# The end of a hybrid decoder layer: part of the last scaling moved to a product with a diagonal matrix

## The chip, the cores and the metric

The kernel runs on one core of a Trainium2 chip. The metric is the time of one execution on the device in microseconds (us), as the median of several runs. Durations of single instructions come from one profiled execution, which has a time of its own.

## What is computed

A decoder layer for 256 tokens of 2048 channels: pre-norm, one wide input projection, two token mixers (a gated delta rule and a block attention), two branch projections merged by gates, an output projection, a post-norm and the residual. What the change touches is the last line alone:

```python
        y = hybrid_mixer(h, w_in[l], ...)          # ends in merged @ w_out
        x = x + rms_norm(y, post_norm_w[l])        # rms_norm: y * rsqrt(mean(y*y) + 1e-6) * w
```

Per token, all 2048 values of y are needed for the mean before any value of the output can be formed.

## The kernel before, in words

The 256 tokens are two tiles of 128 (`t` = 0, 1; a token is a partition). The output projection is cut into four column blocks of 512 (`c` = 0 to 3). Each weight tile is split into a high and a low part of the reduced-precision fp32 form that TensorE takes in one pass, and each product of fp32 operands is three such products (high by high, high by low, low by high); line 147 is the helper that issues all of them. Blocks 0 to 2 are partly formed in combined products earlier; block 3 is plain: for each tile, 16 steps of the contraction by three products, all of tile 0 and then all of tile 1.

**The banks.** Products land in PSUM banks of 128x512 fp32. `acc_tile` takes one from a pool of four, `aux_tile` one from another pool of four. At the end the four `acc` banks hold `c11`, `c21` (block 0, tiles 0 and 1) and `c12`, `c22` (block 1). Block 2 stands in two `aux` banks. Block 3 asks the `acc` pool for two more tiles, `pts`, so these get banks that an earlier block has left; the tile framework adds whatever waits that needs.

**weigh(c, t)** (L1211) reads a finished block twice: ScalarE squares it and sums along the row into `ssy[t][:, c]` (L1214), then VectorE multiplies it by the post-norm weight into `yw[t]` in SBUF (L1215). The two readers of one bank run one behind the other: VectorE's product waits for ScalarE's Square. Blocks 0, 2 and 1 are weighed in this order, the last ones when block 3's weights are already split and kept in SBUF (`keep`, L1246).

**so_far(t)** (L1217) sums the squares of the first three blocks ahead of time.

**finish(t)** (L1224) comes after `weigh(3, t)`: ScalarE takes the root (L1226), VectorE the reciprocal (L1227), and then VectorE goes over the 2048 columns in five pieces (256, 512, 512, 512, 256), each `yw * rs + x` (L1231), with x loaded earlier as `hx`. Behind each piece stands a store to HBM (L1235), in turn on SP's and on ScalarE's DMA queue. For tile 0 this lies beside TensorE's work on tile 1; for tile 1 nothing follows.

**Order.** `mm`, and everything wrapped in `pin`, stays in program order on its engine. Each engine is a queue in order: an instruction that waits holds up all that stand behind it, and a store issued on a queue waits there for its data.

Of the kernel before, what the change touches and what calls it, by code (L numbers as in the profile page):

```python
# [8 lines left out]
F32 = mybir.dt.float32  # L9
F32R = mybir.dt.float32r  # L10
BF16 = mybir.dt.bfloat16
AF = mybir.ActivationFunctionType
ALU = mybir.AluOpType
AX = mybir.AxisListType

P = 128
EPS = 1e-6
# [57 lines left out]
def hybrid_layer(  # L75
# [15 lines left out]
    nc = tc.nc  # L91
    B, S, D = x.shape
    NT = S // P
# [7 lines left out]
    of = out.rearrange("b s d -> (b s) d")  # L101
# [14 lines left out]
    wk = ctx.enter_context(tc.tile_pool(name="wk", bufs=2))  # L116
# [7 lines left out]
    def acc_tile(name):  # L124
        return acc.tile([P, 512], F32, tag="acc", name=name)
# [18 lines left out]
    pin = tc.keep_in_program_order  # L144

    def mm(*args, **kwargs):
        return pin(nc.tensor.matmul(*args, **kwargs))  # L147
# [19 lines left out]
    for c in range(NCH):  # L167
        for t in range(NT):
            cs = slice(c * 512, (c + 1) * 512)
# [7 lines left out]
    ident = cst.tile([P, P], F32, name="ident")  # L177
    make_identity(nc, ident)
    rstd = cst.tile([P, NT], F32, name="rstd")
# [936 lines left out]
    for blk in ORDER:  # L1116
        n, c = blk[:2].rstrip("0123456789"), int(blk[-1])
# [88 lines left out]
    yw = [big.tile([P, D], F32, tag=f"z{t}", name=f"yw_{t}") for t in range(NT)]  # L1206
    hx = big.tile([P, NT, D], F32, tag="g1", name="hx")
    nc.gpsimd.dma_start(hx, xf.rearrange("(t p) d -> p t d", p=P))
    ssy = [cst.tile([P, 4], F32, name=f"ssy_{t}") for t in range(NT)]

    def weigh(c, t, pt):  # L1211
        jy = wk.tile([P, 512], BF16, tag="jy", name=f"jy_{c}_{t}")
        cs = slice(c * 512, (c + 1) * 512)
        pin(nc.scalar.activation(jy, pt, AF.Square, accum_out=ssy[t][:, c : c + 1]))  # L1214
        pin(nc.vector.tensor_tensor(yw[t][:, cs], pt, postw[:, cs], op=ALU.mult))  # L1215

    def so_far(t):  # L1217

        rb = wk.tile([P, 2], F32, tag="mx", name=f"rb_{t}")[:, 0:1]
        pin(nc.vector.tensor_reduce(rb, ssy[t][:, 0:3], axis=AX.X, op=ALU.add))  # L1220
        pin(nc.vector.tensor_scalar(rb, rb, 1.0 / D, EPS, op0=ALU.mult, op1=ALU.add))
        return rb

    def finish(t, rb):  # L1224
        rs = wk.tile([P, 1], F32, tag="rstd", name=f"rs_{t}")
        pin(nc.scalar.activation(rs, ssy[t][:, 3:4], AF.Sqrt, bias=rb, scale=1.0 / D))  # L1226
        pin(nc.vector.reciprocal(rs, rs))  # L1227
        for i, (c0, c1) in enumerate(((0, 256), (256, 768), (768, 1280), (1280, 1792), (1792, D))):
            cs = slice(c0, c1)
            pin(  # L1230
                nc.vector.scalar_tensor_tensor(  # L1231
                    yw[t][:, cs], yw[t][:, cs], rs, hx[:, t, cs], op0=ALU.mult, op1=ALU.add
                )
            )
            (nc.sync if i % 2 == 0 else nc.scalar).dma_start(of[t * P : (t + 1) * P, cs], yw[t][:, cs])  # L1235

    mq.drain()

# [19 lines left out]
    for c, banks in ((0, (c11, c21)), (1, (c12, c22))):  # L1258
        for h in range(2, 4):
            product([quarter(0, h), quarter(1, h)], load(wo, h, c, "y"), banks, [False, False], f"y{c}_{h}")  # L1260
            if h == 2:
                last_parts(c)
        for t in range(NT):
            weigh(2 * c, t, (pts2 if c else banks)[t])
    c = 3
# [3 lines left out]
    for t in range(NT):  # L1269
        weigh(1, t, (c12, c22)[t])  # L1270
    rbs = [so_far(t) for t in range(NT)]
    for t in range(NT):
        for k in range(KT):
            hi, lo = parts[k // 2][0][:, k % 2], parts[k // 2][1][:, k % 2]
            sh = mT[:, k, t * P : (t + 1) * P]
            sl_ = mT[:, k, S + t * P : S + (t + 1) * P]
            mm(pts[t], sh, hi, start=(k == 0), stop=False)
            mm(pts[t], sh, lo, start=False, stop=False)
            mm(pts[t], sl_, hi, start=False, stop=(k == KT - 1))
        weigh(c, t, pts[t])  # L1280
        finish(t, rbs[t])


# [26 lines left out]
```

## Time and profile before

| | us |
|---|---|
| median of 3 runs | 773.82 (773.29 to 774.91) |
| the profiled execution, its own time | 774.99 |
| its span, first to last instruction | 773.2 |
| TensorE products busy | 762.8 |
| VectorE busy | 563.5 |
| ScalarE busy | 433.7 |
| GpSimd busy | 34.6 |

The span is what the profiler saw between the first and the last instruction; the execution's time is 1.8 us longer. In rows of a timeline the first column is the start and the second the duration, both in us; `PE` is TensorE, `PEld` its weight loads, `DVE` VectorE, `ACT` ScalarE, and `SPq` and `ACTq` are the queues on which DMAs are issued. In brackets stands how long the engine had been idle and who released it. In rows of groups the last columns are the summed time in us, the mean of one in ns, and the idle time before.

### The profile page before, as it was taken

The page shows a single profiled execution, that of the slowest core. Times are in us where ns is not written, and L with a number is a line of the kernel's source. Part 1 is how long each engine was busy: PE and PEld are TensorE (multiplying, and loading weights), DVE is VectorE, ACT ScalarE, POOL GpSimd, SP SyncE. Part 2 cuts the span into 40 slices and gives each one's busy share as a digit, 9 for nine tenths or more (in the row PEclk, how much of TensorE's full clock was granted, in tenths as well). Part 3 has the DMA queues.
Part 4 walks back from the last instruction along what each step waited for, and adds up shares of the span by engine and source line. Part 5 has one row for each costly group of instructions (what it writes and reads, how often), then busy time and mean ns, then how long its engine had stood idle before and what let it go on. Part 6 is the DMA issues. An engine that isn't in the chain of part 4 may idle for free.

```text
span 773.2 us, 10375 instructions
## 1 busy us (share of the span) xinstructions
PE 762.8 (99%) x3939; PEld 651.2 (84%) x3939; DVE 563.5 (73%) x912; ACT 433.7 (56%) x652; POOL 34.6 (4%) x63
## 2 busy tenths in 40 slices
PE   8999999999999999999999999999999999999995
PEld 7898998899888888888899888788888888888884
DVE  4786769896977898775457886686658776888753
ACT  4677665566655655454556475654455544556631
POOL 3000001112000000003001000000000000000000
PEclk9999999999999999999999999999999999999999
DMA  8576576548665557569437356657544955375912
GB/s 304 173 217 212 179 219 183 152 137 222 193 210 171 181 200 208 174 186 205 131 109 276 130 193 218 242 201 248 206 163 163 380 174 209 111 293 190 332 54 109
DMA packets 93656, 151.87 MB, mean 196 GB/s; under 512 B 3237, under 2 KB 46886, under 8 KB 93094
## 3 DMA queue, kind: packets, MB, share of 16 engines
q1 hardware_dynamic: 88902, 134.42, 53.7%
q0 software_dynamic: 4128, 15.74, 6.2%
q10 hardware_dynamic: 576, 1.05, 0.4%
q8 instruction: 31, 0.51, 0.3%
q14 instruction: 19, 0.16, 0.1%
HBM read 148.04 MB, written 3.15 MB: 196 GB/s over the span
## 4 chain that ended last, share of the span: by engine, by line
PE 96%; ACT 2%; DVE 1%; DMA 1%; issue 0%; SPq 0%; DVEq 0%
PE a_gb L147 11%; PE a_ga L147 11%; PE a_y L147 11%; PE a_k L147 6%; PE a_zg L147 6%; PE a_mq L147 6%; PE a_v L147 6%; PE a_mk L147 6%; PE a_ub L147 6%; PE a_zm L147 6%; PE a_mv L147 5%; PE a_ua L147 5%; PE a_q L147 4%; PE s L147 1%; PE ms L147 1%; PE po L147 1%
## 5 line engine op out<-in xcount | busy, mean ns | idle before, releaser
L147 PE MATMUL a_ga<-hi_ga,hT 128*128 128x512 f32 x256 | 82.1, 394 | 0.0
L147 PE MATMUL a_gb<-hi_gb,hT 128*128 128x512 f32 x256 | 80.1, 390 | 0.0
L226 DVE TENSOR_TENSOR lo_gb<-raw_gb,hi_gb 128x1024 fp32r<-128x1024 f32 x32 | 38.9, 1224 | 25.0 <-ACT hi_gb L225 24.9
L147 PEld LDWEIGHTS a_gb<-hi_gb,hT 128*128 128x128 f32 x256 | 48.0, 188 | 10.5
L147 PEld LDWEIGHTS a_ga<-hi_ga,hT 128*128 128x128 f32 x256 | 48.1, 188 | 10.0
L225 ACT CAST hi_gb<-raw_gb 128x1024 fp32r<-128x1024 f32 x32 | 33.3, 1051 | 35.5 <-PE a_gb L147 26.5
L225 ACT CAST hi_ga<-raw_ga 128x1024 fp32r<-128x1024 f32 x32 | 33.7, 1055 | 32.3 <-PE a_ga L147 13.7
L226 DVE TENSOR_TENSOR lo_ga<-raw_ga,hi_ga 128x1024 fp32r<-128x1024 f32 x32 | 38.9, 1223 | 17.7 <-ACT hi_ga L225 17.5
L147 PE MATMUL a_ga<-lo_ga,hT 128*128 128x512 f32 x128 | 50.1, 391 | 0.1
L147 PE MATMUL a_gb<-lo_gb,hT 128*128 128x512 f32 x128 | 50.1, 391 | 0.0
L147 PE MATMUL a_zg<-hi_zg,hT 128*128 128x348 f32 (+1 forms) x192 | 47.1, 322 | 0.0
L147 PE MATMUL a_mq<-hT,hi_mq 128*128 128x512 f32 x128 | 47.0, 407 | 0.0
L147 PE MATMUL a_mk<-hT,hi_mk 128*128 128x512 f32 x128 | 46.2, 402 | 0.0
L147 PE MATMUL a_y<-hi_y,mT 128*128 128x512 f32 x144 | 46.0, 392 | 0.0
L147 PE MATMUL a_q<-hT,hi_q 128*128 128x512 f32 x128 | 46.0, 399 | 0.0
L147 PE MATMUL a_v<-hT,hi_v 128*128 128x512 f32 x128 | 45.3, 399 | 0.0
L147 PE MATMUL a_k<-hT,hi_k 128*128 128x512 f32 x128 | 41.8, 410 | 0.0
L147 PE MATMUL a_ub<-hi_ub,obT 128*128 128x512 f32 x128 | 41.3, 395 | 0.0
L147 PE MATMUL a_zm<-hi_zm,hT 128*128 128x512 f32 x128 | 40.5, 392 | 0.0
L147 PE MATMUL a_mv<-hi_mv,hT 128*128 128x512 f32 x128 | 40.1, 390 | 0.0
L147 PE MATMUL a_v<-hT,lo_v 128*128 128x256 f32 x128 | 35.9, 281 | 0.0
L147 PE MATMUL a_q<-hT,lo_q 128*128 128x256 f32 x128 | 35.9, 281 | 0.0
(385 smaller groups left out, 1970.9 us busy)
## 6 DMA issues: line engine op xcount, KB each, us to landing
raw_ga<-in_w_in_dram SPq DMA_DIRECT2D x16, 1024.0 KB, 5.1
raw_gb<-in_w_in_dram SPq DMA_DIRECT2D x16, 1024.0 KB, 6.0
raw_y<-in_w_out_dram SPq DMA_DIRECT2D x15, 1024.0 KB, 5.1
raw_q<-in_w_in_dram SPq DMA_DIRECT2D x8, 1024.0 KB, 5.6
raw_mv<-in_w_in_dram SPq DMA_DIRECT2D x8, 1024.0 KB, 5.0
raw_v<-in_w_in_dram SPq DMA_DIRECT2D x8, 1024.0 KB, 5.8
raw_zm<-in_w_in_dram SPq DMA_DIRECT2D x8, 1024.0 KB, 5.2
raw_mq<-in_w_in_dram SPq DMA_DIRECT2D x8, 1024.0 KB, 5.8
```

The costliest lines, as they stand in the source:

```text
L147: return pin(nc.tensor.matmul(*args, **kwargs))
L225: nc.scalar.copy(hi, raw)
L226: nc.vector.tensor_tensor(lo, raw, hi.bitcast(F32), op=ALU.subtract)
```

## The change

Tile 1's last step is divided. Its columns 0 to 767 are formed by TensorE and ScalarE: two `acc` banks, `r0` (512 columns) and `r1` (256), are filled with x by ScalarE ahead of block 3; when the reciprocal is there, VectorE builds a 128x128 diagonal matrix of it, two products in full fp32 of that matrix with `yw` add the scaled rows onto x in the banks, and ScalarE copies the banks to SBUF. VectorE forms columns 768 to 2047 as before, in three pieces. The five stores of tile 1 are now four on SP's queue and one on ScalarE's, with r0's store between VectorE's second and third piece. Tile 0 is finished as before. Beside it, the factor 1/2048 of the mean moves from the root into the Square's scale, and ScalarE's root is written directly behind the Square.

```diff
-        pin(nc.scalar.activation(jy, pt, AF.Square, accum_out=ssy[t][:, c : c + 1]))
+        pin(nc.scalar.activation(jy, pt, AF.Square, scale=float(D) ** -0.5, accum_out=ssy[t][:, c : c + 1]))
+        if c == 3:
+            root(t)
         pin(nc.vector.tensor_tensor(yw[t][:, cs], pt, postw[:, cs], op=ALU.mult))
...
-        pin(nc.vector.tensor_scalar(rb, rb, 1.0 / D, EPS, op0=ALU.mult, op1=ALU.add))
+        pin(nc.vector.tensor_scalar_add(rb, rb, EPS))
...
+    rs = [wk.tile([P, 1], F32, tag="rstd", name=f"rs_{t}") for t in range(NT)]
+
+    def root(t):
+        pin(nc.scalar.activation(rs[t], ssy[t][:, 3:4], AF.Sqrt, bias=rbs[t]))
+
+    def finish(t):
+        pin(nc.vector.reciprocal(rs[t], rs[t]))
+
+        def scaled(queue, c0, c1):
             cs = slice(c0, c1)
             pin(
                 nc.vector.scalar_tensor_tensor(
+                    yw[t][:, cs], yw[t][:, cs], rs[t], hx[:, t, cs], op0=ALU.mult, op1=ALU.add
                 )
             )
+            queue.dma_start(of[t * P : (t + 1) * P, cs], yw[t][:, cs])
+
+        if t == 0:
+            for i, (c0, c1) in enumerate(((0, 256), (256, 768), (768, 1280), (1280, 1792), (1792, D))):
+                scaled(nc.sync if i % 2 == 0 else nc.scalar, c0, c1)
+            return
+
+        diag = wk.tile([P, P], F32, tag="pT", name="diag")
+        pin(nc.vector.tensor_scalar_mul(diag, ident, rs[t]))
+
+        def copied(queue, pt, c0, c1):
+            cs = slice(c0, c1)
+            pin(nc.scalar.copy(yw[t][:, cs], pt[:, : c1 - c0]))
+            queue.dma_start(of[t * P : (t + 1) * P, cs], yw[t][:, cs])
+
+        for pt, c0, c1 in residual:
+            mm(pt[:, : c1 - c0], diag, yw[t][:, c0:c1], start=False, stop=True, skip_group_check=True)
+        scaled(nc.sync, 768, 1024)
+        scaled(nc.sync, 1024, 1536)
+        copied(nc.sync, *residual[0])
+        scaled(nc.sync, 1536, D)
+        copied(nc.scalar, *residual[1])
...
     rbs = [so_far(t) for t in range(NT)]
+
+    residual = [(acc_tile("r0"), 0, 512), (acc_tile("r1"), 512, 768)]
+    for pt, c0, c1 in residual:
+        pin(nc.scalar.copy(pt[:, : c1 - c0], hx[:, NT - 1, c0:c1]))
     for t in range(NT):
...
         weigh(c, t, pts[t])
-        finish(t, rbs[t])
+        finish(t)
```

In the changed file the Square is L1214, VectorE's product with the weight L1217, the root L1229, the reciprocal L1232, the diagonal matrix L1250, the pieces L1237 with stores L1241, the copies L1254 with stores L1255, and the filling of `r0` and `r1` L1303.

More of the change, by code (lines that the diff above doesn't have):

```diff
@@ L1220, in so_far @@
         pin(nc.vector.tensor_reduce(rb, ssy[t][:, 0:3], axis=AX.X, op=ALU.add))
-        pin(nc.vector.tensor_scalar(rb, rb, 1.0 / D, EPS, op0=ALU.mult, op1=ALU.add))
+        pin(nc.vector.tensor_scalar_add(rb, rb, EPS))
         return rb
[L1224 to L1228, printed above, removed]
+    rs = [wk.tile([P, 1], F32, tag="rstd", name=f"rs_{t}") for t in range(NT)]
[4 more added lines that the diff above has]
+        def scaled(queue, c0, c1):
             cs = slice(c0, c1)
@@ L1231, in finish @@
                 nc.vector.scalar_tensor_tensor(
-                    yw[t][:, cs], yw[t][:, cs], rs, hx[:, t, cs], op0=ALU.mult, op1=ALU.add
+                    yw[t][:, cs], yw[t][:, cs], rs[t], hx[:, t, cs], op0=ALU.mult, op1=ALU.add
                 )
             )
-            (nc.sync if i % 2 == 0 else nc.scalar).dma_start(of[t * P : (t + 1) * P, cs], yw[t][:, cs])
+            queue.dma_start(of[t * P : (t + 1) * P, cs], yw[t][:, cs])
[16 more added lines that the diff above has]
+        copied(nc.scalar, *residual[1])
     mq.drain()
```

## The prediction

> **What bounds the kernel now.** I read the page's chain first, then the chain in order of time for the end, then the timeline around the two places that the diff touches, and last the DMA view of the end.
>
> ```profile
> PE 96%; ACT 2%; DVE 1%; DMA 1%; issue 0%; SPq 0%; DVEq 0%
> ```
>
> ```profile
> 739.92 25.50 PE a_y L147 x112
> ...
> 768.11 1.72 DVE yw L1231 x3
> ```
>
> TensorE is the bound all the way to the last product of column block 3; any pause of TensorE before that lengthens the run one for one. Behind it stands the finish of token tile 1, whose own rows follow (columns: start, duration, both in us).
>
> ```profile
> 765.01 0.40 PE L147 MATMUL a_y<-hi_y,mT 128*128 128x512 f32 x1
> ...
> 765.45 0.60 ACT L1214 ACTIVATE jy<-a_y 128x512 bf16<-128x512 f32 x1 [8.59 <-PE a_y L147]
> ...
> 766.17 0.69 DVE L1215 TENSOR_TENSOR yw<-a_y,postw 128x512 f32<-128x512 f32 x1 [6.20 <-ACT jy L1214]
> 766.77 0.15 DVE L1227 RECIPROCAL rs<-rs 128x1 f32<-128x1 f32 x1
> 766.96 0.49 DVE L1231 SCALAR_TENSOR_TENSOR yw<-yw,rs,hx 128x256 f32<-128x256 f32 x1
> 767.37 0.74 DVE L1231 SCALAR_TENSOR_TENSOR yw<-yw,rs,hx 128x512 f32<-128x512 f32 x1
> 767.48 0.33 SPq L1235 DMA_DIRECT2D out_dram<-yw  x1
> 768.14 0.34 ACTq L1235 DMA_DIRECT2D out_dram<-yw  x1
> 769.35 0.48 DVE L1231 SCALAR_TENSOR_TENSOR yw<-yw,rs,hx 128x256 f32<-128x256 f32 x1
> 769.86 0.33 SPq L1235 DMA_DIRECT2D out_dram<-yw  x1
> ```
>
> The first piece (256 columns) is done at 767.45 and its store is issued 0.03 later; the last is done at 769.83. Five stores of together 1.05 MB follow each other. Whether VectorE or the stores end the run is read from the DMA view of 764 to 774, 40 slices of 0.25 us:
>
> ```profile
> DMA  0000000000000000068099999999880000000000
> GB/s 0 0 0 0 0 0 0 0 0 0 0 0 0 0 0 0 0 229 287 25 369 352 393 393 369 385 385 393 316 295 4 0 0 0 0 0 0 0 0 0
> ```
>
> The first store moves its 131 KB from about 768.35 to 768.75; the second starts at about 768.98; from there to about 771.45 the DMA engines are full without a gap. So data begins about 0.85 us after an issue, and 918 KB take 2.47 us, 371 GB/s. VectorE only decides when this stream starts; once it runs, the stream ends the kernel. The span closes at 773.2, 1.75 us behind the data, which I take as fixed.
>
> **The change part by part.**
>
> *Square, root, mean.* The scale moves from the root into the Square, and the root is written ahead of VectorE's product; the order of instructions on both engines stays, with the same forms. Cost 0.
>
> *The two seeds.* ScalarE copies 768 columns of x into two PSUM banks behind its last Square of block 1 (about 0.9 us by the copy rows below). The row below with 10.23 us of idle time hides them; uncovered they would delay the Square of tile 0, which is on no critical path either.
>
> ```profile
> 754.56 0.60 ACT L1214 ACTIVATE jy<-a_y 128x512 bf16<-128x512 f32 x1 [10.23 <-PE a_y L147]
> ```
>
> *The banks.* This is the part that the diff hides. r0 and r1 come from the pool of four banks that also holds c11, c12, c21, c22 and the two banks of block 3. In the order of the kernel before, block 3's first product waits for nothing. In the changed program's order r0 and r1 receive the banks of c11 and c21, block 3 those of c12 and c22, and its first product (keep_g, tile 0) waits for VectorE. By the count of that semaphore in the built program it waits for the L1217 product that reads c12. All later products of TensorE are queued behind it. What it waits for, in the trace of before:
>
> ```profile
> 743.16 0.39 PE L147 MATMUL a_y<-hi_y,mT 128*128 128x512 f32 x1
> 743.38 0.39 PE L147 MATMUL a_y<-keep_g,mT 128*128 128x512 f32 x1
> ...
> 743.16 0.41 PEld L147 LDWEIGHTS a_y<-keep_g,mT 128*128 128x128 f32 x2
> ...
> 742.96 0.60 ACT L1214 ACTIVATE jy<-a_y 128x512 bf16<-128x512 f32 x1 [2.40 <-PE a_y L147]
> 743.46 0.19 ACT L1214 ACTIVATION_READ_ACCUMULATOR jy<-a_y 128x1 f32 x1
> ...
> 743.69 0.69 DVE L1215 TENSOR_TENSOR yw<-a_y,postw 128x512 f32<-128x512 f32 x1 [0.86 <-ACT jy L1214]
> ```
>
> The Square of c12 ends at 743.65, VectorE starts 0.04 later and is done at 744.38. With the same 0.04 TensorE goes on at 744.42. The price of a cold start, weights and product together, shows here:
>
> ```profile
> 36.57 0.19 PEld L147 LDWEIGHTS a_zg<-hi_zg,hT 128*128 128x128 f32 x1
> 36.57 0.43 PE L147 MATMUL a_zg<-hi_zg,hT 128*128 128x344 f32 x1
> ...
> 36.84 0.32 PE L147 MATMUL a_zg<-lo_zg,hT 128*128 128x344 f32 x1
> ...
> 36.99 0.48 PE L147 MATMUL a_zg<-hi_zg,hT 128*128 128x344 f32 x2
> ```
>
> The second product follows 0.27 after the first, the next 0.15: 0.12 extra. So the first keep_g product really runs from 744.54 instead of 743.38: **+1.16**. Ends: +1.04 if the weights are loaded during the wait, +1.26 if load and product stand one behind the other (743.16 to 743.38). I take the middle value, since its row is a start out of a pause. Nothing later gives this back, since TensorE has no idle time from here to 765.41. Tile 1's wait on c22 is long over when it comes.
>
> The Trainium skill (TensorE: Matmul & The Clock Gate, "Step-by-step: what each phase is for") says that TensorE pulls weight loads ahead of products still running. By it the term would be 1.04 and the sum 0.12 smaller. The trace does load ahead while products run, but shows no pause with a full queue behind it, so I leave it as the lower end.
>
> *The tail*, in the times of before, without that shift. VectorE builds diag at 766.96:
>
> ```profile
> L326 DVE TENSOR_SCALAR dg<-ident,rstd 128x128 f32<-128x128 f32 x2 | 0.5, 278 | 0.0
> ```
>
> ```profile
> 35.11 0.47 DVE L326 TENSOR_SCALAR dg<-ident,rstd 128x128 f32<-128x128 f32 x2
> ```
>
> Two of them take 0.47 and one 0.28, so the next instruction starts 0.19 later. The pieces of VectorE then end at 767.63 (256), 768.31 (512) and 768.97 (512): the first 0.18 later than before, the last 0.86 earlier. Their steps are those of before, 0.41 and 0.66 apart.
>
> TensorE gets diag at 767.24 + 0.04 and runs from 767.40. Its fp32 products:
>
> ```profile
> 359.96 1.50 PE L147 MATMUL po<-mv,pT 128*128 128x128 f32 x12
> 361.21 0.47 PE L147 MATMUL a_mk<-hT,hi_mk 128*128 128x512 f32 x1
> ```
>
> po has three products of 128 columns for each of two heads, and 12 records: two records for one product, 0.104 each. 512 columns are four times that, 0.83, and 256 columns 0.42; no product of that width in full fp32 stands in the trace. Below, it could be two ordinary steps of 0.23, 0.46; above, twice the 0.83 (rival C). I take 0.83, the row's own rate. A product's end lies 0.16 behind its last step (0.39 long, 0.23 apart), so r0 is ready at 768.39 and r1 at 768.81. ScalarE copies them:
>
> ```profile
> L1164 ACT COPY sums_f<-mt 128x512 f32<-128x512 f32 x2 | 1.2, 588 | 1.7 <-DVE mT L1162 1.7
> ...
> L461 ACT COPY y_k<-a_k 128x256 f32<-128x256 f32 x8 | 2.7, 374 | 0.0
> ```
>
> With 0.04 from product to ScalarE (765.41 to 765.45), the copies are done at 769.02 and about 769.35.
>
> Stores: SP issues piece 1 at 767.66 (data from 768.51) and piece 2 at 768.34 (769.19 to 769.90). Third on SP is r0's, at 769.05, data from 769.90: just when piece 2 is through. VectorE's last piece was done at 768.97 but is queued behind it on SP, at 769.40; r1's goes through ScalarE's queue at 769.38. Both have data before 770.3, so from 769.90 the remaining 655 KB run without a gap: 1.77 us, to 771.67 against 771.45: **+0.22**. Ends: -0.22, if everything ran gapless from 768.51 at 385 GB/s; +1.05 by rival C.
>
> **Sum.** 1.16 + 0.22 = 1.38 us on the profiled execution's own 774.99 (span 773.2): 776.4. That run is 1.2 us above the median of the runs shown, 773.82; on the median the sum gives **775.2**, +0.18%. A measurement of this kernel tells about 0.2% (1.55 us) from no change, so this lies just below what can be told.
>
> **The rivals.**
>
> *B, TensorE's wait costs nothing* (not slower): the product that must wait finds its bank read early. For it: the wait is one instruction of 0.69 us. Against: the Square of c12 and then VectorE both stand between c12's last product and the release, and 743.38 is 1.0 us ahead of it. Left is the tail: 773.82 + 0.22 = 774.0, 773.6 by its lower end. It decides as soon as block 3 gets banks that are free before 743.2.
>
> *D, VectorE's earlier end reaches the end of the run* and the wait is absent: the change does what its words suggest. 773.82 - 0.86 = 773.0. Against it speaks the full DMA row from 769 to 771.45.
>
> *C, the fp32 products cost twice 0.83* (clearly slower). r0 is then ready 0.83 later, its store's data starts at 770.73, the stream ends at 772.50: the tail is +1.05, the sum 2.2, the time 776.0. It decides from the moment that r0's copy is later than 769.02; each us beyond is paid in full, since VectorE's last store is queued behind. For it: TensorE has paused for 1.87 us when diag comes. Against it the granted clock:
>
> ```profile
> 766.00:768.00 2.00, 0.00 (x0) 0.00 (x0) 1.80 (x4) 0.43 (x3) 0.00 (x0) 1.00 0.00 0
> 768.00:770.00 2.00, 0.00 (x0) 0.00 (x0) 1.83 (x4) 0.00 (x0) 0.00 (x0) 0.98 0.68 256
> 770.00:771.00 1.00, 0.00 (x0) 0.00 (x0) 0.00 (x0) 0.00 (x0) 0.00 (x0) 0.50 1.02 383
> ```
>
> The clock (the column before the DMA share) is full to 768, 0.98 in the next 2 us and half only from 770, so the products at 767.4 to 768.7 still find it full. The same page of the Trainium skill ("Part 1: The HAM clock gate") puts the drop behind an idle window of about 3.4 us that runs freely; the 4.5 us here agree, and 1.87 us would not fill one. So C keeps a small chance, for other causes more than for the clock.
>
> **How the numbers follow.** Forecast (wait paid, tail about even) 0.72, with its own range 774.7 to 775.9 from the ends of the two terms; as its middle lies 0.17 us under the 0.2% line (775.37), 0.42 of it is within 0.2% and 0.30 slower. C 0.13, slower. B 0.09, within. D 0.06: half within, half faster, and that only by the scatter of the runs. Faster 0.03, same 0.54, slower 0.43. The range reaches from B's forecast down by the scatter of the medians, 773.9, to C with the upper end of the wait and the same scatter, 776.6.
>
> **What would show it.** In the profile after: a pause of TensorE of about 1.1 us ahead of the first keep_g product, released by VectorE's yw product; the block's last product at about 766.6 instead of 765.4; two records each for r0 and r1, together about 1.25 us; ScalarE's copies of 0.59 and 0.37; the stores without a gap over the last 655 KB. Wrong would be: no pause (B), products of 1.7 us (C), a DMA stream that ends earlier against the last product than 6.0 us (D), or any change before 743 us.

## The result and the profile after

The changed kernel takes 775.92 us (median of 8 runs, 774.70 to 776.49) against 773.82 us: a ratio of 1.0024 from all the runs (the two medians alone would give 1.0027), 95% interval 1.0014 to 1.0033. It is slower by about 2 us. That it is slower is clear; whether by more than the 0.2% line of the prediction is not, since the interval has the line inside it. The forecast was 775.2, within a range of 773.9 to 776.6.

The profiled execution took 776.24 us, its span is 774.5. The page's chain by engine, of the changed kernel:

```profile
PE 94%; ACT 2%; DMA 2%; DVE 1%; issue 0%; SPq 0%; ACTq 0%
```

TensorE is still the bound, but the chain now leaves it in two places. The end of the chain in order of time (start, duration, what):

```profile
741.53 0.70 ACT jy L1214 x2
...
742.25 0.70 DVE yw L1217
...
742.99 22.21 PE a_y L147 x96
...
765.23 0.70 ACT jy L1214 x2
...
765.95 0.69 DVE yw L1217
...
766.75 0.30 DVE diag L1250
...
767.18 2.85 PE r L147 x4
...
770.05 0.37 ACT yw L1254
```

**The first place** is the wait on the bank of c12. ScalarE's Square and VectorE's product stand in the chain between two products of TensorE, where before the products ran on without a gap. The timeline at the restart:

```profile
742.99 0.19 PEld L147 LDWEIGHTS a_y<-keep_g,mT 128*128 128x128 f32 x1 [1.31 <-DVE yw L1217]
742.99 0.50 PE L147 MATMUL a_y<-keep_g,mT 128*128 128x512 f32 x1 [0.88 <-DVE yw L1217]
```

The weights and the product start together, 0.04 us after VectorE's end at 742.95. From the Square of c12 to the end of block 3's last product it now takes 741.53 to 765.19, 23.66 us; before it was 742.96 to 765.41, 22.45. The wait costs 1.21 us. The 0.88 in brackets is less, since it counts from the modelled end of the product before; against the Square of c12 the first keep_g product starts 1.04 us later than it did (742.99 less 741.53, against 743.38 less 742.96), and the cold start adds the rest.

```profile
764.79 0.40 PE L147 MATMUL a_y<-hi_y,mT 128*128 128x512 f32 x1
...
767.46 0.99 SPq L1241 DMA_DIRECT2D out_dram<-yw  x2
...
769.20 0.59 ACT L1254 COPY yw<-r 128x512 f32<-128x512 f32 x1 [2.96 <-PE r L147]
769.81 0.33 SPq L1255 DMA_DIRECT2D out_dram<-yw  x1
770.05 0.37 ACT L1254 COPY yw<-r 128x256 f32<-128x256 f32 x1 [0.27 <-PE r L147]
770.23 0.38 SPq L1241 DMA_DIRECT2D out_dram<-yw  x1
770.45 0.34 ACTq L1255 DMA_DIRECT2D out_dram<-yw  x1
```

**The second place** is the tail, here from the end of block 3 at 765.19 to the end of the span: 9.31 us, against 7.79 before (765.41 to 773.2). ScalarE starts to copy r0 at 769.20, 2.16 us after VectorE's end of diag (767.04), where 1.19 had been worked out (768.43 less 767.24), and r1 0.85 later. The stretches of the end show why; behind the five engines' busy times stand the granted clock, the DMA share and GB/s:

```profile
766.00:768.00 2.00, 0.82 (x1) 0.44 (x2) 1.97 (x5) 0.24 (x1) 0.00 (x0) 0.81 0.00 0
768.00:770.00 2.00, 2.00 (x4) 0.67 (x2) 0.75 (x2) 0.59 (x1) 0.00 (x0) 0.50 0.52 197
770.00:771.00 1.00, 0.01 (x1) 0.00 (x0) 0.00 (x0) 0.37 (x1) 0.00 (x0) 0.67 0.36 137
```

A mean of 0.81 over 2 us means full clock for 1.24 us and half for the rest: TensorE's clock fell at 767.24, just as the first product with the diagonal began, and all four records ran at half clock. By the same reckoning (0.67 over the next us) it was back at 770.66, 3.42 us later. In the kernel before it fell at 769.92 by the rows of the prediction, 4.5 us after the last product. What it does to the stores, in the DMA view of 764 to 774 (slices of 0.25 us):

```profile
DMA  0000000000000000077199500039999998100000
GB/s 0 0 0 0 0 0 0 0 0 0 0 0 0 0 0 0 0 258 262 61 377 393 221 0 0 0 156 393 385 353 369 385 299 246 37 0 0 0 0 0
```

The stream that was gapless stands still for nearly 1 us (769.6 to 770.6) while SP's queue waits for r0, with VectorE's finished last piece behind it.

The two together are 1.21 + 1.52 = 2.73 us. The profiled spans differ by only 1.3, because this execution was already 1.43 us ahead at the Square of c12 (741.53 against 742.96). 1.13 us of that lead stands at the first product of prr, whose instructions and those ahead of it are the same in both kernels:

```profile
34.40 0.35 PE L147 MATMUL prr<-dg,ones 128*128 128x128 f32 x1
```

And in the kernel before:

```profile
35.53 0.35 PE L147 MATMUL prr<-dg,ones 128*128 128x128 f32 x1
```

So the difference of two single spans says little here; differences of stages and of medians of many runs say more.

### The profile page after: what moved, and what is told of

It reads as the page before. It is cut to its first block, busy times and chain, and to the rows that moved or that the text cites. A ratio compares the mean times of both kernels' runs of the same rounds, so it can differ in the third digit from the quotient of the medians.

```text
span 774.5 us, 10387 instructions
## 1 busy us (share of the span) xinstructions
PE 764.4 (99%) x3943; PEld 651.1 (84%) x3943; DVE 562.5 (73%) x911; ACT 435.3 (56%) x656; POOL 34.6 (4%) x63
## 4 chain that ended last, share of the span: by engine, by line
PE 94%; ACT 2%; DMA 2%; DVE 1%; issue 0%; SPq 0%; ACTq 0%
PE a_gb L147 11%; PE a_y L147 11%; PE a_ga L147 10%; PE a_zg L147 6%; PE a_mq L147 6%; PE a_v L147 6%; PE a_k L147 6%; PE a_mk L147 6%; PE a_ub L147 6%; PE a_zm L147 6%; PE a_mv L147 5%; PE a_ua L147 5%; PE a_q L147 4%; PE s L147 1%; DMA raw_ga<-in_w_in_dram 1%; PE ms L147 1%
```

## The experiments

Theory: the loss is two things, the wait on the bank and products at half clock behind a pause of TensorE. The ratios of the experiments are to the kernel before, run beside them (medians 773.83 and 773.81); "tail" is the time from the end of block 3's last product to the end of the span.

| kernel | median us | ratio (95%) | Square of c12 to end of block 3 | tail |
|---|---|---|---|---|
| before | 773.82 | | 22.45 | 7.79 |
| changed | 775.92 | 1.0024 (1.0014 to 1.0033) | 23.66 | 9.31 |
| e1 free banks | 774.50 | 1.0010 (1.0001 to 1.0019) | 22.45 | 8.55 |
| e2 kept warm | 775.13 | 1.0018 (1.0009 to 1.0027) | 23.66 | 8.34 |
| e3 both | 774.13 | 1.0001 (0.9992 to 1.0010) | 22.42 | 8.33 |
| e4 wait alone | 775.00 | 1.0012 (1.0004 to 1.0021) | 23.63 | 7.83 |
| e5 changed, again | 776.66 (one run) | | 23.66 | 8.51 |
| e6 stores reordered | 774.11 | 1.0003 (0.9994 to 1.0011) | 22.43 | 8.26 |
| e7 early stream | 773.79 | 0.9997 (0.9988 to 1.0006) | 22.43 | 8.02 |
| e8 the same, no diagonal | 774.29 | 1.0005 (0.9996 to 1.0014) | 22.45 | 8.35 |

**e4, the wait alone.** The kernel before, plus the fillings of r0 and r1, which nobody reads:

```diff
     rbs = [so_far(t) for t in range(NT)]
+    residual = [(acc_tile("r0"), 0, 512), (acc_tile("r1"), 512, 768)]
+    for pt, c0, c1 in residual:
+        pin(nc.scalar.copy(pt[:, : c1 - c0], hx[:, NT - 1, c0:c1]))
```

> The kernel before, with only the two fillings of r0 and r1 added ahead of block 3 (nobody reads them); the end is finished by VectorE as before. Theory (the banks and their wait): TensorE idles ahead of the first keep_g product until VectorE has read c12, 23.7 us from the Square of c12 to the end of block 3, tail 7.8 us as before, time 775.0. Rival (the wait is free): 22.45 us, 773.8.

Measured: 775.00. Its waits of TensorE, and the Square of c12 and the last product of block 3 in its timeline:

```profile
PE a_y L147 <- DVE yw L1215: 0.9, 1, 0.9
```

```profile
740.94 0.60 ACT L1214 ACTIVATE jy<-a_y 128x512 bf16<-128x512 f32 x1 [2.30 <-PE a_y L147]
...
764.17 0.40 PE L147 MATMUL a_y<-hi_y,mT 128*128 128x512 f32 x1
```

740.94 to 764.57 is 23.63 us, with the tail of before. Two copies on an idle engine cost 1.2 us, only because they take two banks from the pool. With no product behind block 3, the clock falls here too, at 766.58 (0.79 over this us), 2.01 after the last product:

```profile
766.00:767.00 1.00, 0.00 (x0) 0.00 (x0) 0.96 (x4) 0.00 (x0) 0.00 (x0) 0.79 0.00 0
```

**e1, free banks.** The changed kernel with block 3 in the other pool:

```diff
-    pts = [acc_tile(f"a_y{c}_{t}") for t in range(NT)]
+    pts = [aux_tile(f"a_y{c}_{t}") for t in range(NT)]
```

> The changed kernel, but block 3's two tiles take banks of the other pool, so that its first product waits for no reader. Theory (the wait on the bank of c12 costs TensorE 1.2 us): no idle time of TensorE before the first keep_g product, 22.4 to 22.5 us from the Square of c12 to the end of block 3 as in the kernel before (23.7 in the changed one), and 1.2 us off the changed kernel's 775.9: 774.7. Rival (the pause is made up or the cost lies elsewhere): 23.7 us stay, 775.9. The tail from the end of block 3 to the end of the span is 8.0 us if the two products with the diagonal meet the full clock and 9.3 if they meet the half clock.

Measured: 774.50, 1.4 us less than the changed kernel; the intervals of the two ratios still overlap a little, so the stage is the firmer evidence. The pause ahead of keep_g is gone and the stage is 22.45 us again. The clock fell in the middle of its products, and the tail lies between the two values that were expected:

```profile
766.00:767.00 1.00, 0.07 (x1) 0.10 (x1) 0.96 (x4) 0.00 (x0) 0.00 (x0) 1.00 0.00 0
767.00:768.00 1.00, 1.00 (x3) 0.45 (x4) 1.00 (x3) 0.00 (x0) 0.00 (x0) 0.89 0.00 0
768.00:769.00 1.00, 1.00 (x3) 0.28 (x1) 0.50 (x1) 0.58 (x1) 0.00 (x0) 0.50 0.65 240
```

**e2, kept warm.** The changed kernel with nine one-pass products into an unused bank behind block 3:

```diff
             mm(pts[t], sl_, hi, start=False, stop=(k == KT - 1))
+        if t == NT - 1:
+            filler = aux_tile("filler")
+            for i in range(9):
+                mm(filler, mT[:, i, 0:P], parts[0][0][:, i % 2], start=True, stop=True)
```

> The changed kernel with nine extra one-pass products (2.05 us, into a bank that nobody reads) between the end of block 3 and the products with the diagonal. Theory (the pause of 2 us lets the clock drop to half, and that doubles the products): granted clock 1.00 through the products, r0's two records 0.85 to 0.9 us apart in all instead of 1.78, the tail from the end of block 3 to the end of the span 8.0 us instead of 9.3; time 774.6 to 775.3. Rival (full-fp32 products of this width are that slow at any clock): records as before at clock 1.00, tail 9.3, time 775.9. TensorE's wait ahead of keep_g stays, 1.2 us.

Measured: 775.13. The clock is 1.00 through the products, which start at 766.45:

```profile
766.45 1.53 PE L147 MATMUL r<-yw,diag 128*128 128x512 f32 x4
```

```profile
767.00:768.00 1.00, 0.98 (x4) 0.34 (x2) 1.00 (x2) 0.42 (x1) 0.00 (x0) 1.00 0.36 129
```

r0's copy is 0.9 us nearer to the end of block 3 than in the changed kernel's trace, and the tail is shorter by 0.97; against e5, a further execution of the changed kernel (below), by only 0.17. The intervals of this ratio and of the changed kernel's overlap, so the times alone do not show that the useless products make the kernel faster; the trace shows that they keep the clock full and the products short. The tail is 8.34, not 8.0.

**e3, both edits.**

> Both of these edits together. If the two causes are all there is and they add: 22.4 to 22.5 us from the Square of c12 to the end of block 3, tail 8.0 us, time 0.2 us over the kernel before: 774.0. If one of the two is a mis-reading, the time stays at 774.7 or above. If the shorter work of VectorE is worth something once both are gone, the time is under 773.6.

Measured: 774.13, no difference from the kernel before that can be told. The two causes add up, and with both away VectorE's saving of 0.86 us gains nothing that can be told; the interval leaves no room for all of it. The end of its block 3, its products with the diagonal and the copies:

```profile
763.47 0.40 PE L147 MATMUL a_y<-hi_y,mT 128*128 128x512 f32 x1
...
765.85 1.53 PE L147 MATMUL r<-yw,diag 128*128 128x512 f32 x4
...
766.98 0.86 ACT L1254 COPY yw<-r 128x512 f32<-128x512 f32 x2 [2.07 <-PE r L147]
```

Four records in 1.53 us at full clock, 2.83 in the changed kernel. Its DMA view of 763 to 773:

```profile
GB/s 0 0 0 0 0 0 0 0 0 0 0 0 0 0 0 29 352 144 180 385 393 156 385 385 340 324 385 401 320 16 0 0 0 0 0 0 0 0 0 0
```

The stream starts 3.1 us after the end of block 3 (766.95), as forecast, and ends at 770.26, after 6.39: the forecast was 6.26, and 6.04 is that of before.

**e5, the changed kernel again**, one more execution, for its clock.

> The changed kernel once more, unaltered, for a second look at the clock. Theory (the clock is judged in windows of 3.4 us whose position differs from run to run; a window in which TensorE is busy for 42% or less halves it, one with 68% or more does not): the clock falls at another moment after the end of block 3 than the 2.05 us of the first look, anywhere between about 1.1 and 5.1 us, and r0's and r1's records are long only after it. Rival (the clock falls a fixed time after the last product): again 2.0 to 2.1 us. The wait ahead of keep_g is there in any case.

```profile
768.00:769.00 1.00, 0.53 (x2) 0.32 (x3) 0.96 (x4) 0.00 (x0) 0.00 (x0) 1.00 0.00 0
769.00:770.00 1.00, 1.00 (x4) 0.49 (x2) 1.00 (x2) 0.36 (x1) 0.00 (x0) 0.71 0.35 127
770.00:771.00 1.00, 0.46 (x2) 0.00 (x0) 0.05 (x1) 0.60 (x2) 0.00 (x0) 0.50 0.70 266
```

Here the clock fell at 769.42, 2.93 us after block 3's end at 766.49, and r0 was through before; the tail is 8.51. So the same kernel can meet the half clock ahead of its products or in the middle of them, by where the clock's windows lie in that run (more on them below).

**e6, stores reordered** (e3 with VectorE's last store ahead of r0's):

```diff
-        copied(nc.sync, *residual[0])
         scaled(nc.sync, 1536, D)
-        copied(nc.scalar, *residual[1])
+        copied(nc.scalar, *residual[0])
+        copied(nc.sync, *residual[1])
```

> The kernel with both cures (free banks, extra products), and the store of VectorE's last piece issued ahead of r0's, r0's on ScalarE's queue. Theory (with both causes gone the tail is set by when the stream of stores starts and by its gaps): the stream starts 3.1 us after the end of block 3 as before this edit, ends 0.1 to 0.2 us earlier than 6.4, and the time is that of the kernel before within 0.3 us: 774.0. Rival (queueing behind r0's copy is what holds back VectorE's gain of 0.86 us): 0.5 us or more earlier, 773.4.

Measured: 774.11, as e3, and the stream was not shorter (6.43). So this order brings no gain either. It is no clean test of the queue order alone, since r1's copy now waits for ScalarE to issue r0's store.

**e7, early stream** (e3, seven fillers, and the product on block 3 moved behind the first pieces):

```diff
-        pin(nc.vector.tensor_tensor(yw[t][:, cs], pt, postw[:, cs], op=ALU.mult))
+        if (c, t) != (3, NT - 1):
+            pin(nc.vector.tensor_tensor(yw[t][:, cs], pt, postw[:, cs], op=ALU.mult))
...
         scaled(nc.sync, 768, 1024)
-        scaled(nc.sync, 1024, 1536)
+        scaled(nc.sync, 1024, 1280)
+        scaled(nc.sync, 1280, 1536)
+        cs = slice(3 * 512, D)
+        pin(nc.vector.tensor_tensor(yw[t][:, cs], pts[t], postw[:, cs], op=ALU.mult))
         copied(nc.sync, *residual[0])
```

> Both cures (seven extra products), and the reciprocal, the diagonal matrix and three pieces of 256 columns stand ahead of VectorE's product on block 3, which only the last piece needs. Theory (the start of the store stream sets the end): first store issued 2.0 us after the end of block 3 instead of 2.25, data from 2.85, end of the stream 5.7 to 5.95 against 6.04 of the kernel before and 6.4 with the cures alone; time 0.1 to 0.4 us under the kernel before, 773.5, so little that it may not be told. Rival (VectorE's or ScalarE's end counts, not the stream's start): 774.0 as with the cures alone.

**e8, early stream without the diagonal** (the kernel before with the same move):

```diff
-        for i, (c0, c1) in enumerate(((0, 256), (256, 768), (768, 1280), (1280, 1792), (1792, D))):
+        cuts = (0, 256, 768, 1280, 1792, D) if t == 0 else (0, 256, 512, 1024, 1536, D)
+        for i, (c0, c1) in enumerate(zip(cuts, cuts[1:])):
             cs = slice(c0, c1)
+            if t == NT - 1 and c1 == D:
+                pin(nc.vector.tensor_tensor(yw[t][:, cs], pts[t], postw[:, cs], op=ALU.mult))
```

> The kernel before, VectorE doing all 2048 columns, but with the reciprocal and four pieces (256, 256, 512, 512) ahead of the product on block 3. First store issued 1.6 us after the end of block 3 instead of 2.07, data from 2.45; VectorE ends when it did, at 4.4, and its last piece of 512 columns leaves by 6.0. Theory (stream start): end of the stream 5.9 to 6.0, time 773.7. If the diagonal is worth anything by itself, the kernel with it and the early stream is 0.1 to 0.3 us faster than this one.

Measured: 773.79 and 774.29. Neither differs from the kernel before by more than the measurement can tell, nor do their two intervals lie apart. The DMA view (763 to 773) of e7 and then of e8, and e8's last two steps on VectorE:

```profile
GB/s 0 0 0 0 0 0 0 0 0 0 0 0 29 340 197 332 193 348 201 385 385 332 344 389 385 328 8 0 0 0 0 0 0 0 0 0 0 0 0 0
```

```profile
GB/s 0 0 0 0 0 0 0 0 0 0 0 0 0 135 328 307 271 90 385 369 385 393 377 107 0 49 369 385 246 0 0 0 0 0 0 0 0 0 0 0
```

```profile
767.15 0.68 DVE L1233 TENSOR_TENSOR yw<-a_y,postw 128x512 f32<-128x512 f32 x1
767.87 0.75 DVE L1235 SCALAR_TENSOR_TENSOR yw<-yw,rs,hx 128x512 f32<-128x512 f32 x1
```

In e8 the stream starts early, but VectorE isn't done until 768.62, 4.87 us after block 3's end at 763.75: I had expected 4.4, and forgot that the product used to fill the time in which VectorE waits for the root. The stream runs dry (the 0 before 49) and ends no earlier. With the diagonal (e7) VectorE ends 0.7 us sooner, the stream has no hole, and the tail is 0.33 shorter than e8's. If the idea of the change is worth something, it is here; but this is one trace of each, e7 also has the fillers, the other banks and smaller pieces, and its tail, 8.02, is still not under the 7.79 of before. Of e7's expectation the time came nearly true, 773.79 against 773.5; the stream's end did not, 6.1 us instead of 5.7 to 5.95.

## Why the prediction was right, and where it was off

- **The whole.** 775.92 lies within the range, but nearer to rival C's 776.0 than to the forecast's 775.2: of the two terms of the sum one was right, and the other came out too small. That the total stayed in the range is owed to an upper end that had been set for C.
- **The wait on the bank: right.** Forecast +1.16, measured +1.21 in the stage, and +1.2 us alone (e4). Its parts stand as worked out, 0.05 short: VectorE's end, 0.04, and a start in which weights and product come together. The Trainium skill's rule (TensorE: Matmul & The Clock Gate, "Step-by-step: what each phase is for"), by which weights are pulled ahead of products in flight, would have given 1.04 if it held for a product that waits; the rows at 742.99 show that they were not loaded during this wait.
- **The tail: mis-sized.** Forecast +0.22, measured +1.52, and +0.72 in e5. At full clock it is +0.54 (e3), at the clock as it falls in each run more. The failing step is the sentence that "the products at 767.4 to 768.7 still find it full". I took the moment at which the clock had fallen in one execution, 4.5 us after the last product, for a fixed delay. It fell 2.05, 2.83, 2.01, 2.93 and 4.5 us after it in the changed kernel, e1, e4, e5 and before.
- **The rule on the clock: read too narrowly.** The Trainium skill (TensorE: Matmul & The Clock Gate, "Part 1: The HAM clock gate") speaks of an idle window, and I concluded that 1.87 us would not fill one. The clock entries in the traces (when each stretch of granted clock begins and how long it lasts) show the windows. Full clock lasted 757.76 us in before, the changed kernel, e1, e4, e5 and e8, 761.17 in e3 and e6, 764.59 in e7 and 768.00 in e2: steps of 3.41 us, each time a whole number of them (222 to 225), and 3.41 us is also the time from fall to return in the changed kernel. So in these traces the clock changed only at the ends of windows of 3.41 us, and the windows lie differently in each run: one ended 2.05 us after block 3 in the changed kernel and 2.93 after it in e5, the same program. The window ahead of the fall in the changed kernel was not idle: it holds 1.37 us of block 3 and 0.06 of r, 42% busy. That e1 and e5 give 42% too adds little, since with a pause of 1.99 us any window that ends between 1.99 and 3.41 us after block 3 holds the same 1.42 us of work; in e4 it is 41%. The window that followed in the changed kernel, 81% busy, ended with full clock. In the kernel before, the window that ended at 766.50 was 68% busy and left the clock alone, and so did one that was 58% busy early in e2 (4.41 to 7.82). Where between 42% and 58% the line lies stays open. No run set the windows' position by hand.
- **Rival C** had the right price for r0, twice 0.83, but I gave it 0.13 and left r1's doubling out. In all three traces with the pause ahead of the products (changed, e5, e1) it came true at least in part, and by the clock, which the prediction had counted against it.
- **The stream of stores: right in kind.** With both causes away, VectorE's 0.86 us are worth nothing that can be told (e3), since the stores begin no earlier and move at about 320 to 400 GB/s in e3's slices from 768.5 to 770.25; D is refuted. Of the +0.54 that remain, 0.35 are the stream (6.39 against 6.04; 0.22 forecast), and 0.2 lie behind it: the span ends 1.94 us after the last data in e3 against 1.75, which I had taken as fixed. e7 and e8 have 1.9 too, e4 and e6 1.8, so it does not follow the diagonal. What lengthens it was not settled.
- **Chances.** Against same 0.54 and slower 0.43, the measured 1.0024 lies on the side of slower, with the 0.2% line still inside its interval. The forecast's own range of 774.7 to 775.9 was missed by a hair. Its upper end does not follow from the ends of the two terms: 1.26 and 0.22 give 775.3, and 1.26 with C's 1.05 gives 776.1.

## What to carry to other kernels

A new buffer in a shared pool moves the others: look in the built order of instructions for waits that were not there, before counting the work that the change adds. When work is given to an engine that has just run out of work, it may find that engine's clock halved; a few useless products in between kept it full here, at no cost that could be told (e2, e3). And an engine's shorter end gained nothing that could be told where a stream of stores behind it was already full. An earlier first store is then the place to try, with the rest of the work keeping the stream fed; here even that (e7, e8) gained too little to be told.

## What was not expected of the hardware

- TensorE's clock can fall 2.0 us after its last product, and in the middle of the products that follow; it came back one window of 3.41 us later, when TensorE had been busy for 81% of it.
- A 256-column store of 128 KB on ScalarE's queue, issued while SP's queue was still moving 512 columns, took 2.8 us from issue to landing; one of the same size on SP's queue, the first of the stream, 1.9. The rows of the changed kernel's DMA issues (the last column is us to landing):

```profile
out_dram<-yw SPq DMA_DIRECT2D x1, 128.0 KB, 1.9
out_dram<-yw ACTq DMA_DIRECT2D x1, 128.0 KB, 2.8
```
